# F and H projections of a hybrid encoder layer as 2x2 block products

## The chip, the cores and the metric

The kernel runs on one core of a Trainium2 chip. The metric is the time of one execution on the device in microseconds (us); lower is better. All numbers of the tensors are fp32.

## The reference, cut to what matters

Two sequences, `x_prompt` and `x_sample`, each 1024 rows of 1024 channels, go through the same layer:

```python
xn = rmsnorm(x, g_pre)
p = xn @ w_in                                      # 1024 x 8192
fv, fg, hv, hg, mg = split(p)                      # 1, 1, 3, 1 and 2 times 1024 columns
fz = real(fftn(fv by 4 groups, axes=(rows, group)))
y_f = (fz * silu(fg)) @ w_fourier_out
v, x1, x2 = split(short_conv(hv, w_short))
z = x2 * long_conv(x1 * long_conv(v, k0), k1)      # by FFT; k0, k1 made by a small network
y_h = (z * silu(hg)) @ w_hyena_out
g_f, g_h = split(sigmoid(mg + b_merge))
out = (g_f * y_f + g_h * y_h) @ w_out
y = x + rmsnorm(out, g_post)
```

The change is in the two products of 1024x1024 by 1024x1024 with `w_fourier_out` (F) and `w_hyena_out` (H), for each of the two sequences, and in what stands around them.

## The kernel before, in words

**Products.** An fp32 product is made of three TensorE products. `split` (L167) rounds an operand to a form with fewer digits, `h`, by a cast on ScalarE (L170), and subtracts `h` from the operand on VectorE or GpSimd (the `sub` of its last argument, L180), which gives the rest `l`. Then h·h, h·l and l·h are summed in PSUM (`mm3`, L193). One matmul has a stationary tile of 128x128 and a moving one of 128x512. L180 is the helper of all element-wise operations with two inputs, so the views tell these apart by the tiles' names.

**Stages.** `_body` (L1588) runs: the setup with the scratch tensors in DRAM (L219 to 228), `phase_fourier` (norms, the projection `fv` and its transform), `phase_main` (L983: input projections `pin`, filters, and the long convolutions), `phase_gates` (L1118) and `phase_out` (L1230). Engines run side by side; a scheduler orders the instructions of each engine by a simulated timeline when the program is built, except where `issue_after` gives an order. A tile waits until its room, named by pool and tag, is free.

**load_x** (L823) reads the normed, transposed sequence from `d_x` into eight pairs of tiles `xh{k}`, `xl{k}` of 128x1024, which stay in SBUF through the projections of a sequence.

**phase_gates** makes the last 11 jobs of the input projection of the second sequence. A job is two column tiles of `w_in`, computed as a 2x2 block product with seven block multiplications in place of eight: `11`, `12`, `s2`, `s3`, `s1`, `s4`, `22`. `s1` to `s4` are sums of the job's weights (`prepare`, L1129), `T1` to `T4` sums of the data blocks, made once (`sums`, L1110). `times` (L1101) is one such multiplication: 4 blocks of k by 3, 12 matmuls. A job's last two multiplications follow the first two of the next job. Results go to `d_g` by `out` (L1173). The weights come through GpSimd's DMA queue (L1134); the sums and the splits' subtractions run on VectorE.

**phase_out** has four units, (sequence, half of its rows). In each, `project` (L1269) makes the 8 tiles of F, then the 8 of H, as plain products: 2 halves of k by 4 by 3, 24 matmuls for one 128x512 tile. `weight` (L1255) loads a weight tile through GpSimd's queue (L1262) and splits it (ScalarE and VectorE). `operand` (L1243) and `ahead` (L1278) load and split the next projection's data, a tile for each tile of the present one. `gated` (L1288) loads a gate, puts it through the sigmoid on ScalarE (L1293) and multiplies the result by it; the F and H parts are added in SBUF and stored to `d_m` (L1377). `beside` (L1302) spreads the loads, splits and sums of `w_out` over units 1 and 2: its blocks stay in SBUF (pool `bl`), two of its sums go to `d_t` and come back in unit 3.

**last_rows** (L1388) makes the output rows in 8 jobs of 2 x 128 rows, each a 2x2 block product of `d_m` and `w_out` in seven multiplications like the gates, then the norm, the residual and the store. Its loads of `d_m` go through GpSimd's queue (L1399).

In the trace TensorE's results are named `pfv`, `pft` (Fourier), `pin`, `pX`, `pT` (main stage), `pg` (gates), `pyf`, `pyh` (F and H) and `po` (output rows). `tpx` (L357) are transposes of the input at the start.

Of the kernel before, what the change touches and what calls it, by code (L numbers as in the profile page):

```python
# [16 lines left out]
P = 128  # L17
# [143 lines left out]
class K:  # L161
# [34 lines left out]
    def setup(self, ctx):  # L196
# [29 lines left out]
        self.d_m = [dt(f"d_m{u}", [P, 4, 8, P]) for u in range(2 * NB)]  # L226
        self.d_t = [dt(f"d_t{j}", [P, 4, 512]) for j in range(2)]
# [595 lines left out]
    def load_x(self, b, ks=range(8)):  # L823
        nc = self.nc
        if 0 in ks:
            self.xh, self.xl = [], []
        for k in ks:
            h = self.xp.tile([P, L], F32R, tag=f"xh{k}", name=f"xh{b}_{k}", bufs=1)
            l = self.xp.tile([P, L], F32R, tag=f"xl{k}", name=f"xl{b}_{k}", bufs=1)
            r = l.bitcast(F32)  # L830
            nc.sync.dma_start(r, self.d_x[b][k])
            self.split(h, l, r, "dve", "act")
            self.xh.append(h)
            self.xl.append(l)

    def inproj(self, sec, mt, b=None):
# [3 lines left out]
        for q in range(2):  # L840
# [15 lines left out]
            for n in range(2):  # L856
                for kk in range(4):
                    k = 4 * q + kk
                    s = slice(512 * n, 512 * n + 512)
                    self.mm3(ps[:, s], (h[:, kk], l[:, kk]), (self.xh[k][:, s], self.xl[k][:, s]), k == 0, k == 7)  # L860
# [122 lines left out]
    def phase_main(self, nct=8, nb=NB, nf=16):  # L983
        tc, nc, a = self.tc, self.nc, self.a
        with ExitStack() as es:
# [19 lines left out]
            nc.gpsimd.tensor_copy(self.cfwd[:, 0, 0:1], self.xl[4][:, 0:1])  # L1005
# [112 lines left out]
    def phase_gates(self):  # L1118

        tc, nc, a = self.tc, self.nc, self.a
        wp, b = self.wp, 1
        jobs = [(s, c) for c in range(0, 8, 2) for s in (0, 4, 5, 6) if (s, c) not in self.PLAIN]
        with ExitStack() as es:
            pool = lambda n: es.enter_context(tc.tile_pool(name=n, bufs=1, reuse_waits="tile"))
            self.open_mm(es, "psg")
            gs, gw, gr = pool("gs"), pool("gw"), pool("gr")
            def prepare(sec, c):  # L1129


                r = gr.tile([P, 4, 512], F32, tag="raw", name="wraw", bufs=2)
                for i in range(2):
                    nc.gpsimd.dma_start(r[:, 2 * i:2 * i + 2].rearrange("p a b -> p (a b)"), a["w_in"][sec, c + i])  # L1134
                s = gw.tile([P, 4, 512], F32, tag="sum", name="wsum", bufs=1)
                A = {}

                def parts(n, pool, tags, src, bufs):
# [479 lines left out]
```

## Time and profile before

| what | value |
|---|---|
| median of 3 runs | 2398.07 us (2398.02 to 2398.45) |
| span of the profiled execution | 2394.9 us, 36369 instructions |
| gates (`pg`), about | 1677 to 1887 us of the span |
| F and H projections (`pyf`, `pyh`) | 1887.4 to 2235.5 us |
| output rows (`po`) | 2235.5 to 2394.9 us |
| bytes moved | 428.33 MB, mean 179 GB/s |
| GpSimd's DMA queue q0 / SP's q1 | 92.94 MB / 333.03 MB |

Times are microseconds of one core unless they are marked ns. The engines are PE (TensorE's matmuls), PEld (its weight loads, which run beside them), DVE (VectorE), ACT (ScalarE), POOL (GpSimd) and SP (SyncE). A line of the groups reads: code line, engine, operation, out<-in by the program's names, partitions x elements and type, xcount | busy us, mean ns of one | idle us of the engine just before them, and what ended most of it. A line of the chain of waits or of a timeline reads: start, duration, engine, tile, line, xcount [how long the engine had waited, and for what]. A line of the windows reads: from:to, length, then busy time and count of PE, PEld, DVE, ACT and POOL, the granted TensorE clock, the DMA engines' busy share, GB/s. A line of the waits reads: who waited, <- for whom: sum of us, count, longest.

### The profile page before, as it was taken

The page shows a single profiled execution, that of the slowest core. Times are in us where ns is not written, and L with a number is a line of the kernel's source. Part 1 is how long each engine was busy: PE and PEld are TensorE (multiplying, and loading weights), DVE is VectorE, ACT ScalarE, POOL GpSimd, SP SyncE. Part 2 cuts the span into 40 slices and gives each one's busy share as a digit, 9 for nine tenths or more (in the row PEclk, how much of TensorE's full clock was granted, in tenths as well). Part 3 has the DMA queues.
Part 4 walks back from the last instruction along what each step waited for, and adds up shares of the span by engine and source line. Part 5 has one row for each costly group of instructions (what it writes and reads, how often), then busy time and mean ns, then how long its engine had stood idle before and what let it go on. Part 6 is the DMA issues. An engine that isn't in the chain of part 4 may idle for free.

```text
span 2394.9 us, 36369 instructions
## 1 busy us (share of the span) xinstructions
PE 2360.9 (99%) x12988; PEld 2053.6 (86%) x12988; DVE 1889.5 (79%) x3397; ACT 1084.2 (45%) x2063; POOL 461.6 (19%) x506
## 2 busy tenths in 40 slices
PE   6999999999999999999999999999999999999998
PEld 5998888888888888888888888888888888888887
DVE  7875787888879999999989999985555456665677
ACT  6654666677643333333322223333443445444444
POOL 3341222222232233230000000023000111112111
PEclk9999999999999999999999999999999999999999
DMA  8636655555665555545444444435544667776553
GB/s 264 219 129 220 204 169 165 171 171 159 204 215 177 172 170 187 176 145 203 150 131 133 137 150 133 143 121 198 165 160 141 211 215 259 251 259 213 166 166 132
DMA packets 221007, 428.33 MB, mean 179 GB/s; under 512 B 23254, under 2 KB 80952, under 8 KB 220570
## 3 DMA queue, kind: packets, MB, share of 16 engines
q1 hardware_dynamic: 193037, 333.03, 43.1%
q0 software_dynamic: 27568, 92.94, 11.5%
q8 instruction: 102, 1.67, 0.3%
q14 instruction: 79, 0.65, 0.1%
q10 hardware_dynamic: 221, 0.04, 0.0%
HBM read 290.12 MB, written 135.79 MB: 178 GB/s over the span
## 4 chain that ended last, share of the span: by engine, by line
PE 94%; DVE 2%; DMA 1%; ACT 1%; issue 1%; POOL 0%; DVEq 0%; ACTq 0%; POOLq 0%; SPq 0%
PE pin L193 41%; PE pg L193 8%; PE pyf L193 7%; PE pyh L193 7%; PE pX L193 7%; PE pT L193 7%; PE po L193 6%; PE pXf L193 3%; PE pfv L193 3%; PE pft L193 1%; PE tph L901 1%; DVE eo L180 0%; PE pQ L193 0%; DMA wr<-in_w_fo 0%; PE pse L193 0%
## 5 line engine op out<-in xcount | busy, mean ns | idle before, releaser
L193 PE MATMUL pin<-xh,wl 128*128 128x512 f32 x1440 | 563.2, 391 | 0.0
L193 PE MATMUL pin<-xl,wh 128*128 128x512 f32 x1440 | 562.8, 391 | 0.1
L193 PE MATMUL pin<-xh,wh 128*128 128x512 f32 x1440 | 561.9, 391 | 0.0
L180 POOL TENSOR_TENSOR wl<-wr,wh 128x512 fp32r<-128x512 f32 x132 | 227.6, 1725 | 1148.7 <-ACT wh L170 1125.4
L193 PEld LDWEIGHTS pin<-xl,wh 128*128 128x128 f32 x1440 | 271.0, 188 | 50.8 <-DVE xl L180 0.4
L193 PEld LDWEIGHTS pin<-xh,wh 128*128 128x128 f32 x1440 | 270.8, 188 | 51.0
L193 PEld LDWEIGHTS pin<-xh,wl 128*128 128x128 f32 x1440 | 271.0, 188 | 50.5
L170 ACT CAST wh<-wr 128x512 fp32r<-128x512 f32 x260 | 161.1, 620 | 333.6 <-PE pin L193 107.8
L180 DVE TENSOR_TENSOR t<-pX,k 128x1024 f32<-128x1024 f32 x128 | 155.6, 1216 | 9.8 <-PE pX L193 6.5
L193 PE MATMUL pX<-bh,cfwd 128*128 128x256 f32 x768 | 162.3, 289 | 0.0
L180 DVE TENSOR_TENSOR wl<-wr,wh 128x512 fp32r<-128x512 f32 x128 | 87.9, 688 | 91.5 <-ACT wh L170 91.5
L193 PE MATMUL pyf<-sf,wh 128*128 128x512 f32 x512 | 157.7, 389 | 0.0
L193 PE MATMUL pyh<-sh,wh 128*128 128x512 f32 x512 | 157.4, 389 | 0.0
L193 PE MATMUL pT<-cinv,yh 128*128 128x256 f32 x768 | 145.3, 284 | 0.0
L193 PEld LDWEIGHTS pT<-cinv,yh 128*128 128x128 f32 x768 | 123.2, 190 | 6.8
L170 ACT CAST bh<-b 128x512 fp32r<-128x512 f32 x144 | 89.1, 620 | 87.3 <-DVE b L180 50.6
L193 PEld LDWEIGHTS pX<-bh,cfwd 128*128 128x128 f32 x768 | 126.4, 190 | 2.2
L193 PEld LDWEIGHTS pyf<-sf,wh 128*128 128x128 f32 x512 | 96.1, 188 | 20.0
L193 PEld LDWEIGHTS pyh<-sh,wh 128*128 128x128 f32 x512 | 96.1, 188 | 20.0
L193 PE MATMUL pT<-cinv,yl 128*128 128x256 f32 x384 | 109.0, 284 | 0.0
L193 PE MATMUL pX<-bl,cfwd 128*128 128x256 f32 x384 | 108.9, 284 | 0.0
L170 ACT CAST yh<-y 128x512 fp32r<-128x512 f32 x96 | 59.4, 619 | 100.9 <-DVE y L180 98.0
(384 smaller groups left out, 5340.6 us busy)
## 6 DMA issues: line engine op xcount, KB each, us to landing
k<-d_k SPq DMA_DIRECT2D x128, 512.0 KB, 4.1
wr<-in_w_in SPq DMA_DIRECT2D x132, 256.0 KB, 3.2
d_g<-gt SPq DMA_DIRECT2D x124, 256.0 KB, 2.6
d_k<-kt SPq DMA_DIRECT2D x128, 128.0 KB, 2.2
d_k<-kt SPq DMA_DIRECT2D x64, 256.0 KB, 2.3
wr<-in_w_fo POOLq DMA_DIRECT2D x64, 256.0 KB, 4.0
g<-d_g SPq DMA_DIRECT2D x64, 256.0 KB, 4.2
wr<-in_w_ho POOLq DMA_DIRECT2D x64, 256.0 KB, 3.9
```

What stands on the lines that cost most here:

```text
L170: self.rounded = nc.scalar.copy(h, src)
L180: return e.tensor_tensor(out, a, b, op=op)
L193: return self.nc.tensor.matmul(out, lhsT, rhs, start=start, stop=stop, skip_group_check=shared)
L901: nc.tensor.transpose(tp[:, q * P:(q + 1) * P], eo[:, e, q], self.ident)
```

## The change

**F and H.** `phase_tail` takes the place of `phase_gates`, `phase_out` and `last_rows`. F and H of each sequence become one *net* each, in the order F and H of the first sequence, F and H of the second. A net is a 1024x1024x1024 product, done as four jobs of two column tiles, each with the gates' seven multiplications of 12 matmuls. The order is by multiplication first: the `11` of the four jobs, then the four `12`, `s2`, `s1`, `s4`, `s3`, `22`: 28 products of 12 matmuls (`product`; its result is `pn` in the trace).

**Data.** The four jobs share a data block. It is split just ahead of its four products into one of four *rooms* (`ROOM`, `block`: the tiles of `load_x`, now in halves), which rotate. A net's four quarters are loaded raw (`load_r`) and summed in place (`sum_r`, VectorE, 128x1024 operations).

**Weights.** A job's weights are loaded whole (`load_w`) and their sums made by GpSimd (`sum_w`: three and later a fourth, 128x512 each). `weight` splits a product's weight five products ahead, except for the first eight; for the last multiplication (p == 6) the subtraction is GpSimd's, and so is that of the last data block.

**Results.** The F net stores its gated result to `d_m`; the H net adds its own there by an accumulating DMA of GpSimd's queue. `load_g` and `open_g` load a gate four products ahead and put it through the sigmoid two ahead.

**Order.** `todo` holds when each of these steps is issued, counted in products; times below 0 lie in the gate stage. The first two products of net 0 stand between `s1` and `s4` of the last gate job.

**Gates and output rows.** Their weight loads go to SP's queue; the splits of `s4` and `22` subtract on GpSimd. `w_out` is copied within DRAM to `d_wo` (eight copies of 0.52 MB); its sums are made in the gate stage (`last_sums`, three on GpSimd, one on VectorE), stored to `d_t` and loaded and split again behind the last net. A job's two halves of `x` and of the output rows lie in other rooms. The order of the output rows' multiplications and the norm's steps stay.

The diff, cut to its core; what it takes out is in the listing above.

```diff
--- setup
-        self.d_m = [dt(f"d_m{u}", [P, 4, 8, P]) for u in range(2 * NB)]
-        self.d_t = [dt(f"d_t{j}", [P, 4, 512]) for j in range(2)]
+        self.d_m = [dt(f"d_m{u}", [P, 8, 512]) for u in range(2 * NB)]
+        self.d_t = [[dt(f"d_t{j}_{k}", [P, 512]) for k in range(4)] for j in range(4)]
+        self.d_wo = [dt(f"d_wo{k}", [P, D]) for k in range(8)]
--- load_x
-            h = self.xp.tile([P, L], F32R, tag=f"xh{k}", name=f"xh{b}_{k}", bufs=1)
-            l = self.xp.tile([P, L], F32R, tag=f"xl{k}", name=f"xl{b}_{k}", bufs=1)
+            self.X = []
+            self.X.append([])
+            for n in range(2):
+                t = self.xp.tile([P, 2, 512], F32R, tag=f"x{n}{k}", name=f"x{n}{b}_{k}", bufs=1)
+                r = t[:, 1].bitcast(F32)
+                nc.sync.dma_start(r, self.d_x[b][k][:, 512 * n:512 * n + 512])
+                self.split(t[:, 0], t[:, 1], r, "dve", "act")
+                self.X[k].append((t[:, 0], t[:, 1]))
--- phase_gates, phase_out and last_rows become phase_tail
+    def phase_tail(self):
+    def prepare(nm, s, c):
+        r = gr.tile([P, 4, 512], F32, tag="raw", name="wraw", bufs=2)
+        for i in range(2):
+            if nm == "g":
+                nc.sync.dma_start(flat(r[:, 2 * i:2 * i + 2]), a["w_in"][s, c + i])
+            else:
+                nc.sync.dma_start(r[:, 2 * i:2 * i + 2].rearrange("p a (b c) -> p (a b) c", c=P),
+                                  self.d_m[s][:, :, P * (c + i):P * (c + i + 1)])
+        A = {}
+        yield A
+        def parts(n, pool, tags, src, bufs, eng="dve"):
+            h, l = [pool.tile([P, 4, P], F32R, tag=t, name=t, bufs=bufs) for t in tags]
+            self.split(flat(h), flat(l), src, eng, "act")
+            A[n] = h, l
+        parts("11", wp, ("wh", "wl"), r[:, 0], 3)
+        parts("12", wp, ("wh", "wl"), r[:, 1], 3)
+        s = gw.tile([P, 512], F32, tag="sum", name="wsum", bufs=1)
+        self.add("dve", s, r[:, 2], r[:, 3])
+        self.add("dve", r[:, 2], r[:, 2], r[:, 0])
+        self.add("dve", r[:, 0], s, r[:, 0])
+        self.add("dve", r[:, 1], r[:, 0], r[:, 1])
+        parts("s2", gw, ("s2h", "s2l"), r[:, 0], 1)
+        parts("s3", gw, ("s3h", "s3l"), r[:, 2], 1)
+        parts("s1", gw, ("s1h", "s1l"), s, 1)
+        yield A
+        parts("s4", gw, ("s4h", "s4l"), r[:, 1], 1, "pool")
+        parts("22", gw, ("a2h", "a2l"), r[:, 3], 1, "pool")
+        yield A
+    def last_sums(k):
+        ra, rb = [cell(xp, f"x1{2 * (k % 2) + i}", f"ws{i}") for i in range(2)]
+        for r, kk in ((ra, k), (rb, 4 + k)):
+            nc.sync.dma_start(flat(r), a["w_out"][kk * P:(kk + 1) * P])
+        self.sub("pool", ra[:, 0], ra[:, 0], ra[:, 1])
+        self.sub("pool", ra[:, 1], ra[:, 1], rb[:, 1])
+        self.stt("dve", rb[:, 1], ra[:, 0], -1.0, rb[:, 1], MUL, SUB)
+        self.add("pool", rb[:, 0], rb[:, 1], rb[:, 0])
+        for j, t in enumerate((ra[:, 0], rb[:, 1], ra[:, 1], rb[:, 0])):
+            nc.sync.dma_start(self.d_t[j][k], t)
+    PH = [("11", "B11"), ("12", "B21"), ("s2", "T2"), ("s1", "T1"), ("s4", "B22"), ("s3", "T3"), ("22", "T4")]
+    ROOM = [(0, 0), (1, 0), (1, 1), (0, 1)]
+    END = 28 * len(nets)
+    def load_r(n, q):
+        nm, b = nets[n]
+        if q in (0, 2):
+            t = gr.tile([P, 4, 512], F32, tag="raw", name=f"r{q}", bufs=2)
+        else:
+            t = [cell(gs, f"T2{(q // 2) * 2 + i}", f"r{q}{i}") for i in range(2)]
+        R[n, q] = t
+        d = self.d_g[b][0] if nm == "f" else self.d_g[b][4] if b else self.d_sh[b]
+        for k in range(4):
+            nc.sync.dma_start(piece(t, k), d[4 * (q // 2) + k][:, 512 * (q % 2):512 * (q % 2) + 512])
+    def sum_r(n, what):
+        r = [wide(R[n, q]) if (n, q) in R else None for q in range(4)]
+        for i in range(2):
+            if what == "T4":
+                self.add("dve", r[2][i], r[3][i], r[2][i])
+                continue
+            self.sub("dve", r[0][i], r[0][i], r[1][i])
+            self.sub("dve", r[1][i], r[1][i], r[3][i])
+            self.stt("dve", r[3][i], r[0][i], -1.0, r[3][i], MUL, SUB)
+    def block(g, k):
+        i, m = ROOM[g % 4]
+        t = cell(xp, f"x{m}{4 * i + k}", f"n{g % 4}{k}", F32R)
+        q = {"B11": 0, "B21": 2, "T2": 3, "T1": 0, "B22": 3, "T3": 1, "T4": 2}[PH[g % 7][1]]
+        self.split(t[:, 0], t[:, 1], piece(R[g // 7, q], k), "pool" if g % 7 == 6 else "dve", "act")
+        blocks.setdefault(g, []).append((t[:, 0], t[:, 1]))
+    def load_w(n, j, q):
+        nm, b = nets[n]
+        if q:
+            t = W23[n, j] = cell(gs, f"T1{j}", "w23")
+        else:
+            t = W01[n, j] = cell(gw, f"st{j}", "w01") if j < 2 else cell(gs, f"T3{j}", "w01")
+        nc.sync.dma_start(flat(t), a["w_fo" if nm == "f" else "w_ho"][2 * j + q])
+    def sum_w(n, j, late):
+        r01, r23 = W01[n, j], W23[n, j]
+        if late:
+            self.add("pool", r01[:, 1], r01[:, 0], r01[:, 1])
+            return
+        s = S1[n, j] = gw.tile([P, 512], F32, tag=("sum", "s1h", "s1l", "u")[j], name="ws1", bufs=1)
+        self.add("pool", s, r23[:, 0], r23[:, 1])
+        self.add("pool", r23[:, 0], r23[:, 0], r01[:, 0])
+        self.add("pool", r01[:, 0], s, r01[:, 0])
+    def weight(s):
+        n, p, j = s // 28, s % 28 // 4, s % 4
+        src = (W01[n, j][:, 0], W01[n, j][:, 1], W01[n, j][:, 0], S1.get((n, j)), W01[n, j][:, 1], W23[n, j][:, 0] if (n, j) in W23 else None, W23[n, j][:, 1] if (n, j) in W23 else None)[p]
+        q = s % 7
+        if q < 3:
+            h, l = [wp.tile([P, 4, P], F32R, tag=t, name=t, bufs=3) for t in ("wh", "wl")]
+        else:
+            t = cell(gs, f"T4{q - 3}", "wpair", F32R)
+            h, l = tri(t[:, 0]), tri(t[:, 1])
+        self.split(flat(h), flat(l), src, "pool" if p == 6 else "dve", "act")
+        W[s] = h, l
...
+    def net_out(s, p, q, op2):
+        nm, b = nets[s // 28]
+        c, m, o = out_of(s)
+        t = wp.tile([P, 512], F32, tag="gt", name="gt", bufs=3)
+        if q is not None:
+            self.tt("dve", t, p, q, op2)
+        self.mul("dve", t, p if q is None else t, G[s])
+        dst = self.d_m[2 * b + m][:, c]
+        if nm == "f":
+            nc.sync.dma_start(dst, t)
+        else:
+            nc.gpsimd.dma_start(dst, t, accum_op=ADD)
+    def product(s):
+        n, p, j = s // 28, s % 28 // 4, s % 4
+        if p == 0:
+            acc[j] = self.psum("mm", 4, "pn")
+        elif p in (1, 5):
+            acc[4 + j] = self.psum("XT"[j // 2], 2, "pn")
+        t = acc[j + 4 * (p in (1, 5, 6))]
+        self.times(t, W[s], blocks[s // 4], p in (0, 1, 5))
+        if p in (0, 3):
+            keep1[j] = gw.tile([P, 512], F32, tag=("s2h", "s2l", "s3h", "s3l")[j], name="kv", bufs=1)
+            nc.scalar.copy(keep1[j], t)
+        elif p == 2:
+            keepu[j] = gw.tile([P, 512], F32, tag=("a2h", "a2l", "s4h", "s4l")[j], name="ku", bufs=1)
+            nc.scalar.copy(keepu[j], t)
+        else:
+            net_out(s, t, {1: keep1[j], 4: None, 5: keep1[j], 6: keepu.get(j)}[p], ADD if p == 1 else SUB)
...
+    todo = {}
+    def at(t, f, *args):
+        todo.setdefault(t, []).append((f, args))
+    for n in range(len(nets)):
+        z, early = 28 * n, n == 0
+        at(z - (7 if early else 12), load_r, n, 0)
+        at(z - (6 if early else 6), load_r, n, 2)
+        at(z - (3 if early else 10), load_r, n, 1)
+        at(z - (3 if early else 12), load_r, n, 3)
+        at(z + (0.5 if early else -2.5), sum_r, n, "T1")
+        at(z + 1.5, sum_r, n, "T4")
+        at(z + 6, load_r, n, 3)
+        for j in range(4):
+            at(z + j - 14 if not early or j < 2 else -2, load_w, n, j, 0)
+            at(z + j - 6 if not early else -1, load_w, n, j, 1)
+            at(z + (j - 2 if not early else (0, 0, 1, 2.5)[j]), sum_w, n, j, False)
+            at(z + j + 5, sum_w, n, j, True)
+    for s in range(END):
+        t = s - 5
+        if s < 8 and s not in (0, 1, 4, 5, 6):
+            t = {2: 0, 3: 2, 7: 2}[s]
+        elif s in (4, 5, 6):
+            t = 2
+        at(t, weight, s)
+        if out_of(s):
+            at(s - 4, load_g, s)
+            at(s - 2, open_g, s)
+    for g in range(END // 4):
+        for k in range(4):
+            at(4 * g - 6 + k, block, g, k)
...
+    for k in range(8):
+        nc.sync.dma_start(self.d_wo[k], a["w_out"][k * P:(k + 1) * P])
...
+    pa, pb, m1 = first(A, Y)
+    for i, job in enumerate(gates):
+        end = i + 1 == len(gates)
+        p2 = part2(gate_out, job, A, Y, pa, pb, m1)
+        for t in (-3, -2, -1):
+            made = next(p2)
+            if end:
+                step(t)
+        pc, u = made
+        A_, pa_ = A, pa
+        if not end:
+            A = prepared("g", *gates[i + 1])
+            pa, pb, m1 = first(A, Y)
+            if 2 <= i < 6:
+                last_sums(i - 2)
+            if i + 2 == len(gates):
+                step(-6)
+        else:
+            for s in range(2):
+                product(s)
+                step(s)
+        self.times(pa_, A_["s4"], Y["B22"], False)
+        gate_out(job, 0, 1, pa_, None, None)
+        if i + 2 == len(gates):
+            step(-5)
+        self.times(pc, A_["22"], Y["T4"], False)
+        gate_out(job, 1, 0, pc, u, SUB)
+        if i + 2 == len(gates):
+            step(-4)
+    for s in range(2, END):
+        product(s)
...
--- _body
-        k.phase_gates()
-        k.phase_out()
+        k.phase_tail()
```

531 lines of the change are left out of this document (200 added, 331 removed).

## The prediction

> **What bounds the kernel now.** First the busy table and the PE clock of the page, then the chain that ended last.
>
> ```profile
> PE 2360.9 (99%) x12988; PEld 2053.6 (86%) x12988; DVE 1889.5 (79%) x3397; ACT 1084.2 (45%) x2063; POOL 461.6 (19%) x506
> ...
> PEclk9999999999999999999999999999999999999999
> ...
> PE 94%; DVE 2%; DMA 1%; ACT 1%; issue 1%; POOL 0%; DVEq 0%; ACTq 0%; POOLq 0%; SPq 0%
> ```
>
> TensorE is busy from end to end and 94% of the chain is TensorE, so a matmul taken out is worth its full pitch and a wait put in costs its full length. The chain in order of time gives the pitch in the stage that the change rewrites:
>
> ```profile
> 1930.88 43.52 PE pyh L193 x192
> 1974.40 43.52 PE pyf L193 x192
> ...
> 2192.00 43.52 PE pyh L193 x192
> 2235.52 149.61 PE po L193 x660
> ```
>
> 192 matmuls take 43.52 us, 0.2267 us each, with no gap between the eight projections. (The 390 ns of a single matmul elsewhere on the page is its latency.) The busy times by stage (PE, PEld, DVE, ACT, POOL, clock, DMA share, GB/s) show what room the other engines have: gates, projections, output rows.
>
> ```profile
> 1677.00:1862.00 185.00, 185.00 (x818) 153.04 (x817) 105.84 (x149) 72.54 (x123) 9.48 (x18) 1.00 0.46 153
> 1887.00:2235.00 348.00, 348.00 (x1537) 288.17 (x1536) 206.74 (x314) 163.33 (x268) 67.91 (x126) 1.00 0.73 236
> 2235.00:2385.00 150.00, 150.00 (x664) 124.20 (x663) 114.12 (x230) 64.85 (x132) 28.25 (x28) 1.00 0.47 154
> ```
>
> In the projections VectorE is 59% busy, ScalarE 47%; GpSimd only issues DMAs there. Where TensorE waited, the list of waits tells:
>
> ```profile
> PE tpx L357 <- DVE x L342: 11.0, 1, 11.0
> ...
> PE pfv L193 <- ACT eh L170: 3.7, 2, 3.2
> ...
> PE pg L193 <- ACT u L1193: 0.4, 1, 0.4
> ```
>
> Nearly all in the first 60 us; at the change from gates to projections 0.4 us.
>
> **The change part by part.**
>
> **1. Fewer matmuls.** Before: 4 units x 2 projections x 8 x 24 = 1536 matmuls. After: 4 nets x 28 products x 12 = 1344; the instruction listing of the changed program shows 1344 on `pn` and elsewhere the counts of before. 192 x 0.2267 = **-43.5 us** on the path. A product is 12 x 0.2267 = 2.72 us, a net 28 x 2.72 = 76.2 us.
>
> **2. The other engines in a net.** Durations from the groups of lines of the projections, and of GpSimd from the page:
>
> ```profile
> L180 DVE TENSOR_TENSOR wl<-wr,wh 128x512 fp32r<-128x512 f32 x124 | 85.2, 688 | 79.3 <-ACT wh L170 79.3
> L180 DVE TENSOR_TENSOR osum<-oraw 128x1024 f32<-128x1024 f32 x4 | 4.9, 1218 | 0.0
> L170 ACT CAST wh<-wr 128x512 fp32r<-128x512 f32 x124 | 77.0, 621 | 157.7 <-PE pyf L193 69.4 <-PE pyh L193 65.1 <-DMA wr<-in_w_fo 12.8
> L1293 ACT ACTIVATE g<-g,bm 128x512 f32<-128x512 f32 x64 | 46.2, 721 | 18.2 <-DMA g<-d_g 17.1 <-DVE wl L180 1.0
> L180 POOL TENSOR_TENSOR wl<-wr,wh 128x512 fp32r<-128x512 f32 x132 | 227.6, 1725 | 1148.7 <-ACT wh L170 1125.4 <-PE pin L193 17.8 <-PE pXf L193 5.5
> ```
>
> ScalarE: 56 casts x 0.62 + 16 sigmoids x 0.72 + 12 copies at about 0.6 = 53 of 76.2 us: room. VectorE and GpSimd must be taken together, as the main stage shows (POOL first, then DVE):
>
> ```profile
> 377.31 3.33 POOL L180 TENSOR_TENSOR wl<-wr,wh 128x512 fp32r<-128x512 f32 x1 [4.01 <-ACT wh L170]
> ...
> 391.54 1.28 POOL L180 TENSOR_TENSOR wl<-wr,wh 128x512 fp32r<-128x512 f32 x1 [3.72 <-ACT wh L170]
> ```
> ```profile
> 377.45 0.69 DVE L180 TENSOR_TENSOR bl<-b,bh 128x512 fp32r<-128x512 f32 x1
> 378.05 0.76 DVE L180 TENSOR_TENSOR b<-bs,xm 128x256 f32<-128x256 f32 x2
> 378.72 0.76 DVE L180 TENSOR_TENSOR b<-xm,bs 128x256 f32<-128x256 f32 x2
> 379.39 1.29 DVE L180 TENSOR_TENSOR T<-pft,ex 128x512 f32<-128x512 f32 x2
> ...
> 392.04 0.17 DVE L765 RECIPROCAL invn<-pn 128x1 f32<-128x1 f32 x1 [1.30 <-PE pn L764]
> ```
>
> The same GpSimd subtraction takes 1.28 us while VectorE idles and 3.33 us while VectorE runs operations with both inputs in SBUF; it ends 1.25 us after VectorE turns at 379.39 to two with an input in PSUM (`pft`). So GpSimd seems to work only while VectorE has no two-SBUF-input operation running. Two such 512-wide operations take 1.29 us, so each next one adds 0.60; a 1024-wide one adds about 1.22 - 0.08 = 1.14. The Trainium skill (SBUF — State Buffer, section "SBUF: two separate sides") calls the port pair that the two engines share an exclusive lock, held for a whole instruction, with the other engine fully blocked; these rows agree, 3.33 against 1.28.
>
> Per net after: VectorE 24 weight and 24 block splits and 12 multiplications by a gate = 60 x 0.60, and 8 sums x 1.14: 45.1 us with two SBUF inputs; 16 operations on PSUM, 9.6 us. GpSimd: 16 weight sums and 8 splits, 24 x 1.28 = 30.7 us. If these exclude each other: 45.1 + 30.7 = 75.8 of 76.2 us. It just fits on average. Weights are ordered five products ahead (13.6 us), so bunching is mostly covered. I take 1 us of wait for each of nets 1 to 3, **+3 us**. Bounds: 0 if all fits; if nothing overlaps, PSUM operations neither, 54.7 + 30.7 - 76.2 = 9.2 a net, 28 in three.
>
> **3. Net 0.** Here the lead is missing: the summed weights sit in rooms that the last gate job frees, and 15 GpSimd adds stand in one chain ahead of the split of weight 11. Let t = 0 be the end of that gate job's `s2` product. 15 products lie between (`s3`, `s1`, 0, 1, `s4`, `22`, 2 to 10), so product 11 is due at 15 x 2.72 = 40.8. VectorE takes the gate output after `s1` at 5.4 + 0.6 and stands at about 10.7 before the last two differences of the data. In its program order 39 operations follow up to weight 11's split: 5 of 1024 and 34 of 512, less 5 on PSUM: 5.7 + 29 x 0.60 = 23.1 us. GpSimd's 15 adds need 19.2. Excluding each other: 10.7 + 23.1 + 19.2 = 53.0, **12 us** late. Weight 8 stands in VectorE's queue ahead of other splits and waits for the chain's fourth add, and those of 9, 10 and 11 for the 10th, 11th and 15th, so I expect TensorE to wait at products 9 and 11. Bounds: 0 if adds run beside VectorE (loads at 11, 11 + 19.2 + 1.3 = 31.5, in time); at 3.33 us an add 11 + 50 + 1.3 = 62.3, 21.5 late. I take 12, nearer the row of 1.28.
>
> **4. The start.** In the changed program's SP order six of the eight copies of `w_out` to scratch (0.52 MB each, dependent on nothing) stand ahead of the third and fourth loads of `w_fv`, and two more ahead of the stores of `xT`. Rows of the start: SP's issues, TensorE, then GB/s in 40 slices of the first 60 us.
>
> ```profile
> 11.89 0.33 SPq L383 DMA_DIRECT2D wfv<-in_w_fv  x1
> ```
> ```profile
> 33.46 0.75 PE L193 MATMUL pfv<-we,eh 128*128 128x260 f32 x4 [3.17 <-ACT eh L170]
> ```
> ```profile
> GB/s 0 170 345 377 405 395 401 414 412 409 399 115 44 151 283 226 307 134 332 351 289 0 36 204 357 282 302 376 256 203 189 344 248 389 311 22 268 278 254 270
> ```
>
> The first loads run at 400 GB/s until about 16.5 us. Six copies are 3.1 MB: at 400 GB/s 8 us, so these weights land near 26 instead of 18, and their matmuls started at 33.46 for another reason, so this is hidden. At half the rate, since a copy reads and writes, they land near 34; with the splits 2 us late, and each later load and store a little more, to 8 us. The order of VectorE changes too (the second scaling moves ahead of the weight sums), which can shorten the 3.17 us wait: lower bound -3. No row shows a copy within DRAM; I take **+3 us**. The skill (DMA: Bandwidth & Descriptors, "Where 436 GB/s comes from") puts the HBM side at about 358 GB/s a core; the row's 414 exceeds that. By it, as an estimate, 6.3 MB read and written take 17.6 us, and the start costs about 4; the sum would be 1 us higher.
>
> **5. At nothing.** Loads that moved from GpSimd's queue to SP's: 236 GB/s before and about as many bytes in a net; SP issues some 60 in 76 us at 0.4 us. The accumulating writes of the H nets are read 40 products later at the earliest; no row shows one, and at ten times the 4 us of a load they still land in time. Gate and output stages: two splits a job move to GpSimd under 19.0 us of matmuls, where VectorE was 57% and 76% busy. Were this cover gone, 2 x 1.28 us a job would show.
>
> Sum on the profiled execution: 2394.9 - 43.5 + 12 + 3 + 3 = 2369.4 us of span. The median of the runs, 2398.07, lies 3.2 above that span: **2372.6 us**.
>
> **Rivals.**
> - *All hidden*: GpSimd's adds find VectorE's gaps and PSUM operations, and the copies hide. For it: VectorE idles 41% in the projections before; the row of 1.28. Against: VectorE's gaps are gone after. 2398.1 - 43.5 + 0 to 3 = 2354.6 to 2357.6 (2351.6 with the start's gain). 20%.
> - *Collision throughout*: net 0 at 21.5, 3 us in each later net, the start at 8: 2393. With milder values 2381 to 2393. 16%.
> - *Slower: VectorE and GpSimd in strict turn in all four nets.* Each net then lasts 85.4 us, 9.2 over its matmuls: 36.8, with net 0's 12 and 3 for the start 2398.1 - 43.5 + 51.8 = 2406.4. It decides from a loss of (43.5 - 15) / 4 = 7.1 us a net. For it: the average fits with 0.4 us to spare only. Against: GpSimd ran under the two PSUM operations at 379.39. 6%.
> - *That the matmuls are not fewer* is excluded by the listing.
>
> **How the numbers follow.** Forecast, 2360 to 2381, 53%; all hidden 20%; collision 16%; within 0.2% (2393.3 to 2402.9, about what a measurement of this kernel can tell from no change) 5%; strict turn 6%. Faster 0.89, same 0.05, slower 0.06. The range 2354 to 2388 leaves out the strict turn, no change, and the ends of two rivals.
>
> **What would show it.** Right: 1344 `pn` matmuls at 0.2267; TensorE waiting for `wh` or `wpair` about 12 us in all at products 8 to 11 of net 0; GpSimd's adds there well over 1.28 us; few waits in nets 1 to 3. Step 2 or 3 is wrong if adds stay at 1.3 us beside a busy VectorE, or if every net shows waits; step 4 if `pfv` waits for `wfv` or not at all. What I may miss is a wait on SP, where one blocked load holds back all behind it.

## The result

The changed kernel takes **2452.77 us** (median of 4 runs, 2447.33 to 2455.28) against 2398.05 us before: 1.0225 times as long, with a 95% interval of 1.0211 to 1.0240. Predicted were 2372.6 us, faster, with a range of 2354 to 2388. The profiled execution has a span of 2450.4 us; predicted was a span of 2369.4, so 81.0 us have to be explained.

From the page of the changed kernel, its busy table and the chain by engine:

```profile
PE 2346.7 (96%) x12796; PEld 2030.5 (83%) x12796; DVE 2010.5 (82%) x3456; ACT 1128.4 (46%) x2201; POOL 650.1 (27%) x526
...
PE 80%; DVE 8%; DMA 6%; ACT 3%; issue 3%; POOL 1%; SPq 0%; DVEq 0%; ACTq 0%; POOLq 0%
```

There are 192 matmuls fewer (12988 to 12796), as forecast. But TensorE holds only 80% of the chain, where it held 94%; most of the rest is VectorE, DMA and ScalarE, on which it waits. The windows of the changed kernel show where. They are cut at the first matmul of each part: the start, the main stage, the gates, nets 0 to 3, the output rows. (Columns as before: length, then busy time of PE, PEld, DVE, ACT, POOL, the granted clock, DMA share, GB/s.)

```profile
0.00:204.00 204.00, 177.64 (x1382) 169.48 (x1383) 147.95 (x345) 118.58 (x255) 66.18 (x90) 0.98 0.66 223
204.00:1683.60 1479.60, 1476.53 (x8476) 1299.74 (x8474) 1300.66 (x2356) 656.79 (x1292) 289.76 (x236) 1.00 0.52 169
1683.60:1893.70 210.10, 205.34 (x902) 168.82 (x902) 120.06 (x164) 84.56 (x149) 44.91 (x33) 1.00 0.54 185
1893.70:1999.10 105.40, 87.86 (x362) 69.65 (x361) 94.18 (x96) 53.95 (x96) 66.82 (x35) 0.94 0.64 217
1999.10:2093.90 94.80, 81.25 (x337) 65.37 (x336) 78.15 (x88) 46.30 (x83) 48.32 (x37) 0.93 0.72 196
2093.90:2181.60 87.70, 79.76 (x337) 64.55 (x336) 72.56 (x81) 47.10 (x85) 43.02 (x28) 0.96 0.64 193
2181.60:2275.70 94.10, 82.36 (x338) 65.17 (x337) 66.64 (x91) 52.23 (x94) 34.12 (x29) 0.95 0.67 182
2275.70:2441.60 165.90, 155.79 (x673) 127.67 (x671) 126.27 (x233) 67.90 (x146) 56.95 (x41) 0.97 0.51 149
```

At 0.2267 us a matmul, net 0 (with the last gate job's two products, 360 matmuls) would take 81.6 us, the other nets 76.2, the output rows 152.3 and the gates 204. So TensorE loses 6 us in the gates, **23.8, 18.6, 11.5 and 17.9 us in the nets, 13.6 us in the output rows**: 91 us. The clock column says that part of the loss is not waiting: it is 0.93 to 0.96 in the nets, and 1.00 in the projections of the kernel before.

Who waits in the nets (all engines, then SP's DMA queue alone):

```profile
ACT g L1303 <- DMA g<-d_g: 102.9, 33, 11.0
POOL d_m L1316 <- DVE gt L180: 58.0, 18, 13.3
...
DVE wpair L180 <- ACT wpair L170: 39.3, 18, 5.9
...
PE pn L193 <- DVE gt L180: 22.9, 9, 8.0
```
```profile
SPq L1232 <- DVE n L180: 69.6, 19, 8.1
SPq L1314 <- DVE gt L180: 56.1, 25, 8.4
SPq L1298 <- DVE gt L180: 41.5, 14, 12.0
SPq L1257 <- POOL wpair L180: 29.4, 9, 8.7
```

It is a ring: TensorE waits for VectorE (`gt` frees a PSUM bank), VectorE for ScalarE's casts, ScalarE stands in sigmoids that wait for a gate to land, and SP issues loads only when VectorE and GpSimd have freed a room (`n`, `gt`, `wpair`). GpSimd in turn stands before the writes of H's results (`d_m`) until VectorE has made them. The list can't tell which link is the cause. Two were in question: VectorE and GpSimd holding each other up, and the gate loads.

What the first does is seen in net 0, GpSimd's weight sums first, then VectorE in the same stretch (rows left out are marked):

```profile
1905.71 7.47 POOL L180 TENSOR_TENSOR ws<-w 128x512 f32<-128x512 f32 x1 [18.18 <-DVE n L180]
...
1917.05 1.73 POOL L180 TENSOR_TENSOR w<-ws,w 128x512 f32<-128x512 f32 x1
1918.74 1.74 POOL L180 TENSOR_TENSOR ws<-w 128x512 f32<-128x512 f32 x1
1920.44 1.75 POOL L180 TENSOR_TENSOR w<-w,w 128x512 f32<-128x512 f32 x1
```
```profile
1911.34 0.69 DVE L180 TENSOR_TENSOR n<-r,n 128x512 fp32r<-128x512 f32 x1
1911.94 0.69 DVE L180 TENSOR_TENSOR gt<-pg,u 128x512 f32<-128x512 f32 x1
...
1915.89 3.44 DVE L180 TENSOR_TENSOR wpair<-w,wpair 128x512 fp32r<-128x512 f32 x2
1919.25 3.48 DVE L180 TENSOR_TENSOR n<-r,n 128x512 fp32r<-128x512 f32 x2
1922.66 1.78 DVE L180 TENSOR_TENSOR wl<-w,wh 128x512 fp32r<-128x512 f32 x1
1924.36 0.68 DVE L180 TENSOR_TENSOR gt<-pn,kv 128x512 f32<-128x512 f32 x1
```

From 1915.89 on both engines advance by one instruction every 1.70 us: VectorE's 0.60 and 1.10 of GpSimd's. They take turns, and VectorE runs at 0.60 / 1.70 of its speed, except on an operation with an input in PSUM (0.68). The Trainium skill (SBUF — State Buffer, section "SBUF: two separate sides") calls the shared port pair an exclusive lock held for the whole instruction; these rows agree. The first add shows that the turns are not always strict: from 1905.71 on VectorE ran its operations at full pace, 0.60 us from one 512-wide start to the next, and the add ended only 1.24 us after VectorE had come to an operation on PSUM (`pg`, 1911.94).

TensorE's longest wait in net 0 comes at product 11, whose weight is split after these sums:

```profile
1945.16 10.34 PE L193 MATMUL pn<-n,wpair 128*128 128x512 f32 x34 [6.27 <-DVE wpair L180]
```

### The profile page after: what moved, and what is told of

The parts are those of the page before. It is cut to its first block, busy times and chain, and to the rows that moved or that the text cites. A ratio compares the mean times of both kernels' runs of the same rounds, so it can differ in the third digit from the quotient of the medians.

```text
span 2450.4 us, 36487 instructions
## 1 busy us (share of the span) xinstructions
PE 2346.7 (96%) x12796; PEld 2030.5 (83%) x12796; DVE 2010.5 (82%) x3456; ACT 1128.4 (46%) x2201; POOL 650.1 (27%) x526
## 4 chain that ended last, share of the span: by engine, by line
PE 80%; DVE 8%; DMA 6%; ACT 3%; issue 3%; POOL 1%; SPq 0%; DVEq 0%; ACTq 0%; POOLq 0%
PE pin L193 39%; PE pg L193 13%; PE pX L193 7%; PE pT L193 7%; PE pXf L193 3%; PE pfv L193 3%; PE pn L193 3%; DVE n L180 2%; DVE gt L180 2%; DMA g<-d_g 2%; PE pft L193 1%; PE tph L902 1%; DVE r L180 1%; DVE wl L180 1%; DMA x<-in_x 1%
## 5 line engine op out<-in xcount | busy, mean ns | idle before, releaser
L193 PE MATMUL pin<-x,wh 128*128 128x512 f32 x2880 | 909.6, 392 | 2.4 <-ACT ktmp L793 2.4
L193 PEld LDWEIGHTS pin<-x,wh 128*128 128x128 f32 x2880 | 536.0, 188 | 104.6 <-ACT ktmp L793 2.6
L193 PE MATMUL pin<-x,wl 128*128 128x512 f32 x1440 | 563.8, 392 | 0.0
L193 PEld LDWEIGHTS pin<-x,wl 128*128 128x128 f32 x1440 | 271.4, 188 | 51.2
L193 PE MATMUL pn<-n,wpair 128*128 128x512 f32 x768 | 195.6, 414 | 44.6 <-DVE gt L180 22.9
L193 PEld LDWEIGHTS pn<-n,wpair 128*128 128x128 f32 x768 | 152.6, 201 | 85.7 <-ACT ku L1331 10.9
L170 ACT CAST wh<-wr 128x512 fp32r<-128x512 f32 x132 | 81.8, 619 | 151.5 <-PE pin L193 91.7
L193 PE MATMUL pn<-n,wh 128*128 128x512 f32 x384 | 118.7, 390 | 3.0 <-ACT ku L1331 1.8
L180 DVE TENSOR_TENSOR bl<-b,bh 128x512 fp32r<-128x512 f32 x144 | 101.8, 712 | 2.9 <-ACT bh L170 2.8
L180 DVE TENSOR_TENSOR n<-r,n 128x512 fp32r<-128x512 f32 x96 | 93.4, 996 | 12.3 <-ACT n L170 12.3
```

The source lines that it names most:

```text
L170: self.rounded = nc.scalar.copy(h, src)
L180: return e.tensor_tensor(out, a, b, op=op)
L193: return self.nc.tensor.matmul(out, lhsT, rhs, start=start, stop=stop, skip_group_check=shared)
```

## The experiments

**The two suspected causes, one at a time and together.** In the first run only the gate loads go, in the second only the weight sums, in the third both.

```diff
-                nc.sync.dma_start(t, self.d_g[b][5 if nm == "f" else 6][c][:, 512 * m:512 * m + 512])
-                nc.scalar.activation(G[s], G[s], AF.Sigmoid,
+                nc.scalar.activation(G[s], gp[:, 0:512], AF.Sigmoid,
```

> The 64 loads of gates in the nets are left out: the sigmoid reads a tile that is in SBUF (so the gates' values are wrong); the sigmoids, the multiplications and their rooms stay. Queue theory: the gate loads stand on SP behind loads whose rooms are not free yet, ScalarE waits 103 us in the nets for them with its casts behind it, and that makes most of the 72 us that TensorE loses between the first product of net 0 and the first output row (382.0 us for 114 products of 2.72 us). Then the loss falls below 25 us and the time to 2390 to 2410 us. Theory of the prediction's rival (VectorE and GpSimd in turn, in every net): the two engines have the same work as ever, the loss stays above 50 us and the time above 2430 us.

```diff
     def sum_w(n, j, late):
-                s = S1[n, j] = gw.tile([P, 512], F32, tag=("sum", "s1h", "s1l", "u")[j], name="ws1", bufs=1)
-                self.add("pool", s, r23[:, 0], r23[:, 1])
...
+                S1[n, j] = r23[:, 1]
```

> The 64 sums of weights that GpSimd makes in the nets are left out: the products take unsummed weights instead (so the result is wrong); loads, splits, gates and products stay. Theory of the turns: VectorE's 92 data splits take 1.01 us each in the nets instead of 0.69 because GpSimd holds it up; without the sums they go back to 0.7 to 0.75 and the loss of 72 us falls below 25 us, the time to 2390 to 2410 us. Queue theory: the loads still wait for their rooms in turn; the loss falls by 10 to 25 us only, the time to 2430 to 2445 us.

> Both cuts at once: no weight sums and no gate loads in the nets (the result is wrong in both ways). If the two causes lie beside each other, the gains add up: 2452.8 - 45 - 21 = 2387 us, and the nets last 78 us each. If they are two sides of the same waits, it stays at 2400 to 2408 us, as without the sums alone. What is left beyond 2398.1 - 43.5 = 2354.6 us is the start, the gates' entry and the output rows (7, 4 and 14 us lost in the changed kernel).

Measured: **2431.9, 2407.6 and 2385.0 us** (one run each), from 2452.8. Without gate loads 20.9 us are gained, without sums 45.1, without both 67.8, which is the two added up (66.0) within the spread of single runs. So neither theory alone was right: they lie beside each other, the sums twice as dear as the gate loads. Where the gains lie: without the sums net 0 falls from 105.4 to 85.4 us, the nets 1 and 2 to 81.3 and 78.2, while net 3 keeps 90.5; without the gate loads net 0 stays (105.6). So 20 us of what the sums cost lie in net 0. Of the 48 us lost in nets 1 to 3, 26.6 go with the sums, 21.1 with the gate loads and 42.1 with both. Windows of net 0 and net 1 without gate loads, then without sums:

```profile
1894.40:2000.00 105.60, 89.01 (x361) 71.03 (x360) 96.29 (x96) 50.85 (x91) 66.35 (x35) 0.94 0.54 182
2000.00:2087.40 87.40, 79.69 (x338) 64.55 (x337) 79.65 (x88) 48.75 (x88) 43.53 (x36) 0.96 0.62 161
```
```profile
1893.70:1979.10 85.40, 82.26 (x361) 67.41 (x360) 72.59 (x101) 54.19 (x96) 14.30 (x8) 1.00 0.80 276
1979.10:2060.40 81.30, 78.38 (x337) 64.02 (x336) 60.46 (x84) 46.00 (x83) 23.63 (x21) 0.98 0.77 215
```

and nets 1 and 2 with both gone:

```profile
1975.30:2051.40 76.10, 76.10 (x337) 63.05 (x336) 58.87 (x84) 45.73 (x83) 23.00 (x21) 1.00 0.68 172
2051.40:2127.60 76.20, 76.20 (x338) 63.07 (x337) 59.80 (x86) 46.48 (x84) 16.26 (x12) 1.00 0.62 189
```

There TensorE never waits. The 28 products at 76.2 us, on which the forecast stood, are reached as soon as the other engines keep up; net 0 (84.4 us) and net 3 (82.1) still lose 3 and 6 us in this run. VectorE's busy time in net 1 is 78.2 us for 88 instructions in the changed kernel and 60.5 for 84 without the sums, 0.89 and 0.72 us each: some 15 us are time that GpSimd made it stand.

**Sums on VectorE.** If the turns are the cause, GpSimd's help is worth less than nothing: in the rows above a sum holds VectorE for 1.10 us, and it would cost it 0.60 to make.

```diff
-                self.add("pool", s, r23[:, 0], r23[:, 1])
+                self.add("dve", s, r23[:, 0], r23[:, 1])
```

> The 64 weight sums of the nets run on VectorE instead of GpSimd; nothing is left out. Theory of the turns: a sum costs VectorE 0.60 us, and it no longer loses the time that GpSimd holds it up; a net has 54.7 + 9.6 = 64.3 us of VectorE and 8 GpSimd splits (10.2 us) for 76.2 us of matmuls. Then most of the 45 us come back that the run without sums gained: 2405 to 2425 us. If instead the chain matters (a weight must be summed before it is split, on whichever engine), VectorE has more work and nothing is gained: 2440 us and more.

The second run also moves the eight GpSimd splits of each net (`"pool" if p == 6 else "dve"` and `"pool" if g % 7 == 6 else "dve"` become `"dve"`).

> As the run with the sums on VectorE, and in the nets the last data block's and the last multiplication's splits subtract on VectorE as well, so that GpSimd computes nothing in the nets but for the last net's preparation of the output rows. VectorE has 64.3 + 8 x 0.60 = 69.1 us of 76.2 in a net. Theory of the turns: as fast as the run with the sums alone on VectorE or up to 10 us faster, 2400 to 2420 us. If VectorE is now the bound, slower than that run by 5 to 20 us.

Measured: **2421.99 us** (1.0101 times before, 1.0085 to 1.0118) and **2415.13 us** (1.0075, 1.0060 to 1.0090). Taking work from GpSimd and giving it to the busier engine gains 30.8 and 37.6 us. In nets 1 to 3, which shorten by 11.6, 6.6 and 10.5 us in the first run, what costs is where the sums are made, and not that a weight must be summed before it is split. In net 0 it is the other way round: there only 4.2 of the 20.0 us come back (its window in the first run below), and the rest stays with the sums on either engine. One rival is not excluded in nets 1 to 3: the edit also takes the sums out of GpSimd's queue, where they can stand behind the writes that waited 58.0 us. That the turns themselves cost VectorE time is shown by its splits of the data, in the changed kernel and in the second run:

```profile
L180 DVE TENSOR_TENSOR n<-r,n 128x512 fp32r<-128x512 f32 x92 | 90.8, 1010 | 12.3 <-ACT n L170 12.3
```
```profile
L180 DVE TENSOR_TENSOR n<-r,n 128x512 fp32r<-128x512 f32 x107 | 72.2, 697 | 5.3 <-ACT n L170 5.3
```

1010 ns fall to 697, for the same instruction. What stays is net 0, in which VectorE now has everything to do without a lead; window of net 0 of the first run, then of the second:

```profile
1893.70:1994.90 101.20, 88.00 (x361) 70.59 (x360) 91.14 (x129) 56.58 (x99) 13.92 (x8) 0.92 0.66 230
```
```profile
1890.00:1989.10 99.10, 87.44 (x362) 70.14 (x361) 89.78 (x134) 56.90 (x99) 0.00 (x0) 0.93 0.67 234
```

**Queues for the loads.** The prediction had named SP as what it might miss. One run sends the nets' weight loads, as before the change, through GpSimd's queue (`nc.gpsimd.dma_start` in `load_w`), on the changed kernel; the other sends the gate loads there (in `load_g`), on the run with all of the nets on VectorE.

> The 32 weight loads of the nets go back to GpSimd's DMA queue, as the weights of F and H had it before; the rest stays. Queue theory: SP loses its waits for the weights' rooms (53 us in the nets by the list of waits), gate loads come earlier, and the time falls by 20 to 50 us. If GpSimd's own waits for the same rooms hold up its sums instead, the gain is eaten and the time stays within 15 us of 2453. Theory of the turns: nothing is gained, GpSimd issues 32 more transfers of about 0.9 us, the time rises by 0 to 20 us.

> As the run with all of the nets' sums and splits on VectorE, and the 64 gate loads of the nets go through GpSimd's DMA queue, which has hardly anything else to do there. Queue theory: the part of the loss that the run without gate loads showed (21 us, nets 1 to 3) comes back in addition, 2385 to 2400 us. If the gate loads were late only because VectorE freed rooms late, nothing more is gained: within 5 us of the run with all on VectorE.

Measured: **2454.8 us** (one run) and **2421.33 us** (1.0100, 1.0082 to 1.0118), against 2452.8 and 2415.1 without these edits. No gain in either. The nets take 383.9 us in the first run's profile, 382.0 in the changed kernel; in the second, nets 0 and 2 take 100.7 and 79.3 us, against 99.1 and 80.1. So in these two nets the theory that gate loads stand behind other loads falls. In nets 1 and 3 GpSimd's queue has waits of its own, 94.7 us before the writes of H, and the run does not decide there. The waits of the second run suggest why nothing is gained (GpSimd and ScalarE in the nets):

```profile
POOL g L1298 <- DVE gt L180: 78.6, 8, 40.1
ACT g L1303 <- DMA g<-d_g: 78.1, 37, 7.0
```

The gate loads wait for their own rooms. There are six, and a room comes free when VectorE has multiplied by the gate six results back; load (4.3 us to landing) and sigmoid start only then, on whichever queue. That the gate loads cost some 21 us is shown; how much of it is the issue, the landing, their share of the DMA engines or the sigmoid's place on ScalarE stays open.

**The start.** The copies of `w_out` are issued behind the last load of `xraw` (`with tc.issue_after(raw.ins)`).

> The eight copies of w_out within DRAM are held behind the last load of xraw in the gate stage; nothing else is changed in the code, though the scheduler's order of the start then differs. In the changed kernel the first pin matmul starts at 204.0 us against 199.1 before, and the last at 1683.4 against 1676.7. If the copies cost the start these 6.7 us, the time falls by about 7 us, to some 2446 us; the copies may give 1 or 2 us back in the gates. If the order of VectorE at the start is to blame and not the copies, it stays at 2453 us. The nets should lose as much as in the changed kernel under either theory.

Measured: **2451.5 us** (1.0222, 1.0205 to 1.0239): 1 us gained where 7 were expected, and that is within the noise. The first matmuls of the main stage, before, changed and with late copies (from and to are those of the queried window):

```profile
L193 PE MATMUL pin<-xh,wh x8: 388/389/401, 199.1 to 206.0; 128*128 128x512 f32 x8
```
```profile
L193 PE MATMUL pin<-x,wh x4: 390/399/401, 204.0 to 205.0; 128*128 128x512 f32 x4
```
```profile
L193 PE MATMUL pin<-x,wh x8: 388/394/401, 202.2 to 206.0; 128*128 128x512 f32 x8
```

In the profiles of all versions this point lies between 201.1 and 205.3 us with the copies ahead (ten) and between 198.1 and 203.1 with late copies (five); the means are 203.1 and 200.6. The copies cost the start some 2.5 us, which one run can't tell from its spread.

**Mending.** Four runs that start from the one with the nets on VectorE. *Entry of the rows*: the first loads of `x`, for which SP waited up to 11.9 us in the changed kernel, are issued behind the loads of the sums of `w_out`, and the splits of T2 and B22 subtract on VectorE. *Early sums*: net 0's 16 sums are made by GpSimd in the gate stage and stored. *All three*: both, with late copies. *Sigmoid late*: the same, with `at(s - 1, open_g, s)` for `at(s - 2, open_g, s)`.

```diff
+                    with tc.issue_after(self.summed.ins):
                         nc.sync.dma_start(x[j], a[f"x{b}"][where[j]:where[j] + P, :])
```
```diff
                         last_sums(i - 2)
+                    if 6 <= i < 10:
+                        first_sums(i - 6)
```

> As the run with all of the nets' sums and splits on VectorE, and the entry of the output rows eased: the loads of x for the first rows, whose rooms the last gates still hold, are issued behind the loads of the sums of w_out (SP stood 11.9 us before one of them in the changed kernel, with loads of T1 behind it), and the splits of T2 and B22 subtract on VectorE. If that queue is what holds up s3 and s1 of the first row job (13 us lost in the output rows in every run so far), the output rows fall from 165.5 to about 155 us and the time to 2403 to 2408 us. If it is the accumulating writes and GpSimd's order, 160 us and more stay, and the time at 2411 us or above.

> As the run with all of the nets' sums and splits on VectorE, but the 16 weight sums of net 0 are made by GpSimd in the gate stage, where it has room, stored, and loaded as they are. Step 3 of the prediction (net 0 starts without lead, its sums stand in one chain with VectorE's splits) says that net 0, which loses 17.4 us there, then loses less than 8, and the time falls to 2402 to 2408 us. If SP's queue with 16 more loads is the next limit in net 0, it loses 12 us and more, and the time stays at 2410 us or above.

> The eased entry of the output rows, the early sums of net 0 and the late copies of w_out together. If each of the three does what its own run is to show, 2415 - 10 - 10 - 2 = 2393 us, below the kernel before (2397.9); if two of them share a wait, 2400 us.

> As the run with all three, and each gate's sigmoid is issued one product later (one product ahead of its use instead of two), so that a gate that lands late holds up fewer of the casts that stand behind it on ScalarE. Queue theory: the nets 1 to 3, which lose 18 us in the run with everything on VectorE, lose 5 to 10 us less, and the time falls by as much against the run with all three. If ScalarE's wait is not on the path any more, the two agree within 3 us.

Measured: **2408.79** (1.0043, 1.0027 to 1.0059), **2411.28** (1.0051, 1.0034 to 1.0068), **2397.96** (0.9996, 0.9986 to 1.0005) and **2396.99 us** (0.9992, 0.9983 to 1.0002). Early sums shorten net 0 from 99.1 to 89.5 us; TensorE loses 7.9 there, just under the 8 that was expected from step 3's mechanism. But the gates grow by 5.9 us in that execution, so that 4 us are left of the gain. The eased entry takes its gain in net 3 (84.2 to 77.7 us) and only 2.4 us in the output rows. All three together reach the kernel before. That is 5 us short of the expected sum, and 5.7 us more than the three gained in their own runs (6.3, 3.9 and 1.3 us). A later sigmoid changes nothing that can be told in this version; whether its place on ScalarE cost something in the changed kernel was not tried.

**The output rows.** Some 10 us were still lost there in the last of these runs. Its ScalarE timeline shows the copy `u`, on which `s1` waits, behind casts for later multiplications and a square:

```profile
2229.91 0.62 ACT L170 CAST s4h<-wraw 128x512 fp32r<-128x512 f32 x1 [5.12 <-DVE gt L180]
...
2237.88 0.63 ACT L1451 ACTIVATE sq<-o 128x512 f32<-128x512 f32 x1 [4.75 <-DVE o L180]
...
2239.02 0.57 ACT L1177 COPY u<-pg 128x512 f32<-128x512 f32 x1
```

The first cast waits behind VectorE, which stood 1.68 us before a room for a result (`gt`) whose accumulating write had not landed. One run issues these casts behind `u`; the other writes without accumulating, so the F part of the result is lost.

```diff
+                if i == 0:
+                    with tc.issue_after(self.kept_u.ins):
+                        list(prep)
+                        load_sum("T4")
```
```diff
-                nc.gpsimd.dma_start(dst, t, accum_op=ADD)
+                nc.gpsimd.dma_start(dst, t)
```

> As the run with all mended and the sigmoids late, and in the first row job the splits of s4, 22 and T4 are issued behind the copy u of s2's partial result, on which s1 waits, instead of ahead of it. In that run u was copied at 2239.0 us, 9 us after s2's last matmul, behind ten casts and a square on ScalarE, and s1 began 7 us late with its first matmuls slow. If that order is the cause, the output rows fall from 162.8 to about 154 us and the time to 2388 to 2391 us, below the kernel before (2398). If the accumulating writes are the cause, less than 3 us are gained.

> As the run with all mended and the sigmoids late, but the H nets write their result to scratch without adding it to the F nets' (the F part is lost, so the result is wrong). If the accumulating writes (5.5 us from issue to landing, a plain one 2.6 us) hold up VectorE by its three rooms for results, the waits in nets 1 and 3 and at the entry of the rows shrink and the time falls by 5 to 12 us. If ScalarE's order is the cause, the output rows stay at 160 us and more and the time within 3 us of the other.

Measured: **2392.86 us** (0.9977, 0.9967 to 0.9986; 10 runs) and **2388.1 us** (one run, of a kernel whose runs spread by 8 us). In the profiled executions each shortens the output rows, from 162.8 to 158.6 and 158.3 us, so both theories seem to hold a part of the same wait, and the order does not give the 8 us that were expected of it. The first is a version that beats both kernels, by 0.23% and 2.4%. Its windows of nets 1 to 3 and the output rows, where 6, 4, 1 and 6 us are still lost:

```profile
1982.60:2065.20 82.60, 77.94 (x337) 64.12 (x336) 69.78 (x108) 45.35 (x81) 10.19 (x12) 0.98 0.78 216
2065.20:2145.40 80.20, 77.73 (x338) 63.89 (x337) 70.25 (x109) 48.86 (x87) 3.73 (x5) 0.98 0.71 224
2145.40:2222.30 76.90, 76.89 (x337) 63.17 (x336) 62.05 (x101) 50.63 (x90) 9.52 (x11) 1.00 0.79 213
2222.30:2381.10 158.80, 154.73 (x673) 126.92 (x671) 123.99 (x239) 67.99 (x147) 50.57 (x37) 0.99 0.52 157
```

## Why the prediction was wrong, point by point

- **Step 1, fewer matmuls (-43.5 us): right.** 1344 `pn` matmuls at 0.2267, and nets of 76.2 us once nothing is in the way.
- **Step 2, the other engines in nets 1 to 3 (+3 us): this step failed.** The mechanism was right: operations with two SBUF inputs and GpSimd exclude each other, and the sum of both came to 75.8 of 76.2 us. The wrong conclusion was "It just fits on average" and 1 us a net. Measured are 18.6, 11.5 and 17.9 us, 48 in all, beyond even the upper bound of 28, which counted the work of two engines and nothing else. Without the gate loads the three nets lose 26.9 us, about that bound; without the sums they lose 21.4, with the sums on VectorE 19.3, without either sums or gate loads 5.9. So the step had two terms wrong: the pair VectorE and GpSimd, put at 3 us, and the gate loads, put at nothing, which cost nearly as much here. Why the pair loses its full overlap and not its average is argued, not shown: two in-order queues without slack, in a ring with ScalarE and SP, hand each lateness on. The 5.9 us left lie in net 3, beside the preparation of the output rows; the eased entry took 6.5 us out of that net.
- **Step 3, net 0 (+12 us): right in mechanism, mis-sized.** 23.8 us are lost, 21.5 was the upper bound. GpSimd's chain of adds runs as described, mostly at about 1.70 us an add, but it starts 17.3 us after `s2` (whose last matmul ended at 1888.4 us), where the prediction had put 11, and its first add takes 7.47 us. TensorE waits at products 2, 5, 9, 10 and longest at 11 (6.27 us); by then 17.9 us are lost, where 12 were expected. The other 5.9 come at product 27, which waits 3.76 us for a `gt`. 20 of the 23.8 go with the sums.
- **Step 4, the start (+3 us): about right.** The main stage began 4.9 us later; some 2.5 of it are the copies. The wait is the one that was named: `pfv` waits 5.8 us for `we`, the splits of `w_fv`. With late copies it does not wait for `we` at all, but 3.6 us for `eh`, as before the change (3.7).
- **Step 5, at nothing: wrong for the gates and the output rows.** The queue move of the nets' weights cost nothing (2454.8 against 2452.8 us with them moved back). But the gate loads, which no step priced, cost 20.9 us, and the gates and the output rows lose 6 and 13.6 us. In the output rows ScalarE's order and the accumulating writes seem to make a part of it. In the gates no cause was tried. In the trace the first matmul waits 1.78 us for ScalarE's copy of the last `pin` (L883), which stands behind a cast that waited 2.39 us for VectorE; in the other profiles that wait is 1.2 to 9.9 us, and the kernel before has none there.
- **Not in the sum at all: the clock.** Matmuls at 0.3 to 0.7 us in place of 0.2267 make 19.9 of the 91 us, counted from the starts of the changed kernel's matmuls after 1600 us. They stand behind the waits, above all the longer ones (see below).
- **The rivals.** "Strict turn in all four nets" (6%) named a part of what happened, with 36.8 + 12 us in the nets where 72 were lost; it left out the clock, the gate loads and the output rows. 2406.4 us was still 46 us low. The stated ground against it, that GpSimd ran under the PSUM operations, is true of those operations (0.68 us at 1924.36), but they are only 9.6 us of a net.
- In numbers, from the predicted span of 2369.4: start and main stage +3.7 (6.7 measured, 3 in the sum), gates +6, net 0 +11.8, nets 1 to 3 +45, output rows +13.6 and the end +1.7 make 82 us for the 81.0 to be explained.

## What to carry to other kernels

Before giving work to GpSimd, count it as time taken from VectorE: with both queues full a 512-wide add cost VectorE 1.10 us on GpSimd here, and would have cost 0.60 on VectorE itself. In this kernel such help could pay only where VectorE had real gaps or worked from PSUM. When the sum of two engines that exclude each other comes to 99% of the stage, do not write "it fits"; take the full collision as the forecast. Here that would have given 28 us for nets 1 to 3, and without the gate loads 26.9 were lost. And a stage shortened on the bottleneck engine shortens the time in which all others must do the same work: check every one of them, their loads and the rooms they share, at the new length; the gate loads were not checked here.

## What the runs showed of the hardware that was not expected

**Waits slow the matmuls behind them.** Two rows of TensorE in the changed kernel, 13 matmuls without and 12 after a wait:

```profile
2028.81 3.11 PE L193 MATMUL pn<-n,wpair 128*128 128x512 f32 x13
...
2039.16 4.49 PE L193 MATMUL pn<-n,wpair 128*128 128x512 f32 x12 [3.13 <-ACT ku L1331]
```

The twelve should take 2.88 us by the pitch of the thirteen; they take 1.61 more. In the changed kernel, from 1600 us on, each of the seven waits of 3.13 us and more is followed by 7 to 12 matmuls at about half pace (0.427 us in place of 0.227), 1.5 to 2.5 us in all. Two of 2.13 and 2.76 us were so too, two of 2.25 and 3.06 were not (nor was one of 3.34 in the second run with the sums on VectorE), and shorter ones cost 0.1 us beside themselves. The Trainium skill (TensorE: Matmul & The Clock Gate, section "Part 1: The HAM clock gate") has the array fall to half its clock after an idle window of about 3.4 us that runs freely; the trace agrees on the half, and shows that a wait of 2.13 us can be enough. By these rows a wait over 3 us is, in most cases, to be priced at its length and 1.5 to 2.5 us more.

**Accumulating writes land late, but not by the accumulating alone.** DMA issues of the nets, the plain stores of F and the accumulating ones of H (KB each, median us from issue to landing); the writes of H without accumulating, from the last run; and the copies within DRAM:

```profile
d_m<-gt SPq DMA_DIRECT2D x32, 256.0 KB, 2.6
...
d_m<-gt POOLq DMA_DIRECT2D x32, 256.0 KB, 5.7
```
```profile
d_m<-gt POOLq DMA_DIRECT2D x32, 256.0 KB, 4.5
```
```profile
d_wo<-in_w_out SPq DMA_DIRECT2D x8, 512.0 KB, 9.5
```

An accumulating write of H keeps its room twice as long as a plain store of F (5.7 against 2.6 us). But the two also go through different queues: on GpSimd's queue a plain write took 4.5 us, an accumulating one 5.9 in the run that differs in nothing else. So only about 1.4 us go with the accumulating; the rest of the gap comes with the queue and what runs beside it, which no run here tells apart.
